# Making the gate tiles in one pass, and starting the first partial sums before the root is known

## The chip, the cores and the metric

The kernel runs on one core of a Trainium2 chip. It is written for five engines that run side by side: TensorE (PE in the profile, with its weight loads as PEld), VectorE (DVE), ScalarE (ACT), GpSimd (POOL) and SyncE (SP), which here only issues loads and stores. The metric is the time of one execution on the device in microseconds; lower is better. The median of three runs is compared.

## The reference

One step of a one-layer decoder for 256 prompt tokens and 8 groups of 4 sample tokens, 288 columns in all. Cut to what the change touches:

```python
mod = (silu(c) @ w_ada + b_ada).reshape(n, 6, 1, 2048)
sh_m, sc_m, gt_m, sh_f, sc_f, gt_f = [mod[:, i] for i in range(6)]
h = rms(x, g_mix) * (1 + sc_m) + sh_m
proj = h @ w_in                       # 2048 -> 9216 = 72 tiles of 128
b_gate, c_gate, hc, u, v, ga, gb = split(proj, [1024, 1024, 1024, 1024, 1024, 2048, 2048])
ya = b_gate * causal_conv(c_gate * hc)
yb = gelu(u) * spatial_mix(rms(gelu(v), g_v))
x = x + gt_m * ((sigmoid(ga) * (ya @ w_pa) + sigmoid(gb) * (yb @ w_pb)) @ w_out)
```

Behind it stand a second norm, a gated feed-forward layer of width 5632 and a last norm. `rms(x, g)` divides each token by the root of its mean square over 2048 features; that root is one number per token. Tokens lie along the columns: x is 16 feature tiles of 128 rows by 288 columns. There are nine conditioning vectors: one for the prompt, eight for the sample groups.

## The kernel before

Every large product is made in full fp32 accuracy from two rounded parts: a weight tile of 128x128 is split into `hi` (ACT, L331) and `lo` (VectorE, L333), the activations likewise, and each weight tile takes three matmuls (L344 to L346) of 288 columns.

Weights arrive in blocks of up to 1 MB, in one stream, in the order of the list `steps`. A block goes into one of RAW = 5 raw buffers; its load is issued when the block RAW places ahead of it in the stream is run, and waits on SP until that one's buffer is free (for a weight block: once its `lo` parts are made; for a conditioning block: once its matmuls are done). Blocks are split one ahead of use, in four buffers each for `hi` and `lo`.

Conditioning (`Ada`, L249) is made on TensorE in units: aA gives feature tile 0 of shift and scale, aB tiles 1 and 2, aC tiles 3 to 6, aD tile 7, aE tiles 8 to 15; a2 to a5 serve later stages. A block of it is four column groups of the array side by side (L274). `tail` copies a unit's sum out (L289), transposes it on TensorE (L293 or L298) and adds the bias (L302).

The product `h @ w_in` is split over features, because the conditioning arrives feature by feature. For all 72 output tiles:

- wA: feature 0, six blocks of 12 tiles; `sinkA` copies the 72 partial tiles out, on ACT and VectorE in turn (L434, L436).
- wB: features 1 and 2, nine blocks of 8 tiles; `sinkB` adds (L439).
- wC: features 3 to 7, 24 blocks of 3 tiles; `sinkB` again.
- wD: features 8 to 15, 36 blocks of 2 tiles; `sinkD` adds (L447) and goes on by tile number: 0 to 23 are the convolution's three parts, 24 to 31 u, 32 to 39 v, 40 to 71 the two gates (a tanh, L457).

Before wA come the loads of c, constants, x and aA in this order (L717 to L719), the squares of x (ACT, L150) and their sum (VectorE, L155), the root (`token_rstd3`: L167, a power on POOL, L171), its broadcast over partitions (L177), `norm1`, and `mk_h1(0, 1)`, which scales and shifts feature tile 0 (`modulate`: ACT L205, POOL L208 and L209, ACT L211, VectorE L216). The other 15 tiles are multiplied by the root on POOL (`norm1b`, L410).

The compiler of the program orders each engine's instructions by the program's order and by what it holds to be ready; `tc.issue_after(i)` puts an engine's instructions behind `i` on that engine, without a wait.

Of the kernel before, what the change touches and what calls it, by code (L numbers as in the profile page):

```python
# [10 lines left out]
P = 128  # L11
D = 2048
T = 288
# [6 lines left out]
SLOTS = 92  # L20
RAW = 5
# [24 lines left out]
    "wA": (0, 1, 12),  # L46
    "wB": (1, 2, 8),
    "wC": (3, 5, 3),
    "wD": (8, 8, 2),
# [12 lines left out]
def decoder_kernel(tc, d):  # L62
    nc = tc.nc
    from contextlib import ExitStack
# [12 lines left out]

def _body(tc, nc, d, pc, pw, pslot, ptmp, pps):
# [25 lines left out]
    SY.dma_start(ct, d["c"])  # L104
    cp1 = const("cp1", [P, C1_END])
    SY.dma_start(cp1, d["cpack1"])
# [7 lines left out]
    ident = cp[:, C_ID : C_ID + 128]  # L114
# [6 lines left out]
    def load_x():  # L121
        for a, b in ((0, 5), (5, 10), (10, 14), (14, 16)):
            SY.dma_start(x[:, a:b, :], d["x"][:, a:b, :])
        SY.dma_start(cp, d["cpack2"])
        SY.dma_start(masks[96:], d["cpack2"][:32, C_MASKS : C_MASKS + 32])
# [8 lines left out]
    A.activation(ctt, ct, AF.Tanh, scale=0.5)  # L134
    V.scalar_tensor_tensor(ctt, ctt, 1.0, ct, ALU.add, ALU.mult)
    V.tensor_scalar(cs[:, :, :NC], ctt, 0.5, None, ALU.mult)
# [7 lines left out]
    class SquareSum:  # L144
        def __init__(self):
            self.acc, self.last = None, None

        def add(self, a):
            q = tmp() if self.last is not None else ptmp.tile([P, T], F32, tag="acc", name=nm("acc"), bufs=1)
            A.activation(q, a, AF.Square)  # L150
            if self.last is not None:
                if self.acc is None:
                    self.acc = self.last
                else:
                    V.tensor_tensor(self.acc, self.acc, self.last, ALU.add)  # L155
            self.last = q
# [31 lines left out]
    def split(a, n=T):  # L188
        hi = slot(F32R, (P, n))
        A.copy(hi, a)  # L190
        lo = slot(F32R, (P, n))
        V.tensor_tensor(lo, a, hi.bitcast(F32), ALU.subtract)  # L192
        return hi, lo

    def normed(kt, rb):
        t = slot()
        V.tensor_tensor(t, x[:, kt, :], rb, ALU.mult)  # L197
        return t

    def modulate(ks, get, gm, sh0, out):  # L200
        hs, his = {}, {}

        def affine(k, t):
# [5 lines left out]
            G.tensor_tensor(sam(h[:, TP:]), sam(h[:, TP:]), bc4(mod[:, sh0 + k, 1:]), ALU.add)  # L209
# [34 lines left out]
    class Step:  # L244
        defer = False
        raw = None
        parts = None

    class Ada(Step):  # L249
# [15 lines left out]
        def run(self):  # L265
# [4 lines left out]
            for k in range(self.nk // ks):  # L270
                for j in range(4):
                    kt = self.blk * self.nk + k * ks + j % ks
                    o = (k * 4 + j) * w
                    self.last = PE.matmul(  # L274
                        acc[32 * j : 32 * j + 32, :w],
                        cs[:, kt, :],
                        self.raw[:, o : o + w],
                        start=(kt < ks),
                        stop=(kt >= 16 - ks),
                        tile_position=(0, 32 * j),  # L280
                        skip_group_check=True,
                    )
# [26 lines left out]
    class Blk(Step):  # L309
        def __init__(self, name, idx, rhs, sink):  # L310
            self.name, self.idx, self.rhs, self.sink = name, idx, rhs, sink
# [7 lines left out]
        def split(self, most=99):  # L319
# [4 lines left out]
            for s in range(len(self.parts), n, per):  # L324
# [6 lines left out]
                A.copy(hi, self.raw[:, s * 128 : e * 128])  # L331
# [5 lines left out]
        def run(self):  # L337
            for j in range(self.nm):
                ps = psmain()
                for k in range(self.nk):  # L340
# [3 lines left out]
                    PE.matmul(ps[:, :T], wh, ah, start=first, stop=False)  # L344
                    PE.matmul(ps[:, :T], wh, al, start=False, stop=False)  # L345
                    PE.matmul(ps[:, :T], wl, ah, start=False, stop=last)  # L346
                self.sink(self.idx * self.nm + j, ps)

# [37 lines left out]
    S = {}  # L386

    def squares1():
        ss = SquareSum()
        for k in range(16):  # L390
            ss.add(x[:, k, :])
        S["ss1"] = ss

    def rstd1():
        with tc.issue_after(aA[1].last.ins):
            S["r1"] = token_rstd3(S["ss1"], D)

    def norm1():
        with tc.issue_after(aA[3].last.ins):
            ps = rstd_bcast(S["r1"])  # L400
        with tc.issue_after(S["bc"].ins):
            aA[3].tail()
        S["rb1"] = ptmp.tile([P, T], F32, tag="rb", name=nm("rb"), bufs=1)
        A.copy(S["rb1"], ps)
        xn[0] = normed(0, ps)

    def norm1b():
        for k in range(1, 16):
            xn[k] = slot()
            G.tensor_tensor(xn[k], x[:, k, :], S["rb1"], ALU.mult)  # L410

    xn = {}
    h1 = {}

    def mk_h1(k0, k1):
        def f():
            V.scalar_tensor_tensor(  # L417
                gm1[:, k0:k1, :],
                mod[:, 16 + k0 : 16 + k1, :],
                1.0,  # L420
                gmix[:, k0:k1].unsqueeze(2).to_broadcast([P, k1 - k0, NC]),
                ALU.add,
                ALU.mult,
            )
            modulate(range(k0, k1), xn.pop, gm1, 0, h1)

        return Do(f)
# [3 lines left out]
    def sinkA(m, ps):  # L431
        part[m] = slot()
        if m % 2:
            A.copy(part[m], ps[:, :T])  # L434
        else:
            V.tensor_copy(part[m], ps[:, :T])  # L436

    def sinkB(m, ps):
        V.tensor_tensor(part[m], ps[:, :T], part[m], ALU.add)  # L439
# [5 lines left out]
    def sinkD(m, ps):  # L445
# [10 lines left out]
        elif m >= 40:  # L456
            A.activation(a, a, AF.Tanh, scale=0.5)  # L457
        elif m >= 16:
            mix_conv(m - 16)

# [116 lines left out]
    def sink_wo(m, ps):  # L577
# [8 lines left out]
        for k in range(2 * m - 16, 2 * m - 14) if m >= 8 else ():  # L586
            a = tmp(TU)
            A.activation(a[:, :TP], x[:, k, :TP], AF.Copy, scale=gm2[:, k, 0:1])
            G.tensor_tensor(sam(a[:, TP:T]), sam(x[:, k, TP:]), bc4(gm2[:, k, 1:]), ALU.mult)
            G.tensor_copy(a[:, T : T + NC], mod[:, 48 + k, :])  # L590
            G.memset(a[:, T + NC :], 0.0)
            xg[k] = split(a, TU)
# [77 lines left out]
    aA = ada("aA")  # L670
# [3 lines left out]
    wA = [Blk("wA", i, rh1, sinkA) for i in range(6)]  # L674
    wA[0].defer = True
    wB = [Blk("wB", i, rh1, sinkB) for i in range(9)]
    wC = [Blk("wC", i, rh1, sinkB) for i in range(24)]
    steps += weave(wA, visits(ada("aB"), 2, mk_h1(1, 3)), 1, 4)
    steps += weave(wB, visits(ada("aC"), 4) + visits(ada("aD"), 2, mk_h1(3, 8)), 0, 6)
    steps += weave(wC, visits(ada("aE"), 4, mk_h1(8, 16)), 2, 17)  # L680

    def wD(m0, m1):
        return [Blk("wD", i, rh1, sinkD) for i in range(m0 // 2, m1 // 2)]

    steps2 = wD(32, 40) + wD(24, 26) + [Do(v_stats)] + wD(26, 28) + [Do(v_transpose)] + wD(28, 32)
# [3 lines left out]
    steps2 += weave(wD(40, 72), [[spatial(g)] for g in range(8)], 2, 12)  # L689
    steps2 += [Blk("pa", i, ya.__getitem__, sink_pa) for i in range(8)]  # L690
# [26 lines left out]
    load_x()  # L717
    for s in stream[:AHEAD]:
        s.load()  # L719
    blks = [s for s in stream if isinstance(s, Blk)]  # L720
    nxt, cur = 0, 0
    for s in steps:
# [4 lines left out]
        if i + AHEAD < len(stream):  # L727
            stream[i + AHEAD].load()
# [122 lines left out]
```

## Time and profile before

| | |
|---|---|
| median of 3 runs | 1660.55 us (1659.83 to 1661.02) |
| the profiled execution | 1658.19 us, span 1656.2 us |
| granted TensorE clock, mean | 0.996 |
| moved by DMA | 357.59 MB, 216 GB/s over the span |

The span is what the trace covers. Busy time of TensorE is modelled from pipelined matmuls, so two that overlap count once; the number of matmuls in a stretch says more than the busy share. A row of the timeline has start, length, engine, line, operation, what is written and read, and the count of instructions that were merged; in square brackets stands the engine's idle time before it and what ended that.

### The profile page before, as it was taken

The numbers are of one execution on the slowest core, as the hardware profiler recorded it, in microseconds if no ns is written. First come the engines' busy times: TensorE is split into PE (matmuls) and PEld (weight loads), VectorE is DVE, ScalarE is ACT, GpSimd is POOL, SyncE is SP. The second block draws the span as 40 slices with busy tenths as digits, with TensorE's granted clock in tenths as the row PEclk, the third lists the DMA queues.
The fourth block names the chain that finished last, engine by engine and source line by source line (L and its number), as shares of the span: only waits on it lengthen the run. The fifth ranks groups of instructions, "written<-read, shape, count | busy, mean of one in ns | idle before, by whom it ended". The sixth has DMA issues, their size and how long they took to land.

```text
span 1656.2 us, 31141 instructions
## 1 busy us (share of the span) xinstructions
PE 1624.6 (98%) x12456; PEld 1556.0 (94%) x12456; DVE 995.4 (60%) x2034; ACT 736.2 (44%) x1371; POOL 63.9 (4%) x154
## 2 busy tenths in 40 slices
PE   5999999999999999999999999999999999999997
PEld 5889899989898999999999899999999999999997
DVE  5767556878755557557844455555555555555565
ACT  4534334643444434446733344444444444344453
POOL 3000001000000000002300000000000000000000
PEclk9999999999999999999999999999999999999998
DMA  7685786567777776674466755443454444645342
GB/s 267 254 335 207 277 313 246 191 233 261 277 308 277 282 286 251 251 263 154 152 255 254 304 170 196 171 163 137 158 206 163 168 141 156 204 161 171 126 170 76
DMA packets 56034, 357.59 MB, mean 216 GB/s; under 512 B 6369, under 2 KB 8577, under 8 KB 22737
## 3 DMA queue, kind: packets, MB, share of 16 engines
q1 hardware_dynamic: 55536, 354.88, 58.8%
q8 instruction: 97, 1.59, 0.4%
q0 software_dynamic: 352, 0.73, 0.1%
q14 instruction: 49, 0.39, 0.1%
HBM read 352.50 MB, written 3.09 MB: 215 GB/s over the span
## 4 chain that ended last, share of the span: by engine, by line
issue 50%; DVE 0%; ACT 0%; POOL 0%; PE 0%; POOLq 0%; DVEq 0%
DVE x L651 0%; PE px L177 0%; ACT t L205 0%; ACT s L211 0%; POOL t L208 0%; ACT hi L331 0%; POOL t L209 0%; POOLq L837 0%; DVE s L197 0%; DVE s L216 0%; DVEq L837 0%; POOLq L208 0%
## 5 line engine op out<-in xcount | busy, mean ns | idle before, releaser
L344 PE MATMUL pm<-s,hi 128*128 128x288 f32 x3712 | 1100.1, 297 | 7.2 <-ACT s L434 3.1
L345 PE MATMUL pm<-s,hi 128*128 128x288 f32 x3712 | 1097.1, 296 | 0.1
L346 PE MATMUL pm<-s,lo 128*128 128x288 f32 x3712 | 1094.1, 295 | 0.0
L331 ACT CAST hi<-raw 128x512 fp32r<-128x512 f32 (+1 forms) x966 | 581.9, 610 | 793.0 <-PE pm L345 661.7
L333 DVE TENSOR_TENSOR lo<-raw,hi 128x512 fp32r<-128x512 f32 (+1 forms) x966 | 652.5, 682 | 450.7 <-ACT hi L331 434.7
L344 PEld LDWEIGHTS pm<-s,hi 128*128 128x128 f32 x3712 | 698.8, 188 | 26.7 <-issue 14.6
L346 PEld LDWEIGHTS pm<-s,lo 128*128 128x128 f32 x3712 | 699.2, 188 | 0.2 <-DVE lo L333 0.2
L345 PEld LDWEIGHTS pm<-s,hi 128*128 128x128 f32 x3712 | 698.8, 188 | 0.5 <-DVE s L216 0.5
L274 PE MATMUL ada<-raw,cs 128*32 128x512 f32 (+2 forms) x960 | 91.1, 519 | 12.3 <-DMA raw<-in_aA 12.2
L439 DVE TENSOR_TENSOR s<-pm,s 128x288 f32<-128x288 f32 x144 | 64.3, 454 | 48.4 <-PE pm L346 48.2
L274 PEld LDWEIGHTS ada<-raw,cs 128*32 128x32 f32 x960 | 29.0, 113 | 56.4 <-issue 39.0
L447 DVE TENSOR_TENSOR s<-pm,s 128x288 f32<-128x288 f32 x72 | 32.8, 455 | 24.1 <-PE pm L346 23.8
L190 ACT CAST s<-t 128x288 fp32r<-128x288 f32 (+1 forms) x76 | 32.9, 432 | 21.0 <-DVE t L550 9.6
L192 DVE TENSOR_TENSOR s<-t,s 128x288 fp32r<-128x288 f32 (+1 forms) x76 | 34.8, 458 | 7.1 <-ACT s L190 7.0
L171 POOL TENSOR_TENSOR r<-r,mhalf 128x3 f32<-128x3 f32 x4 | 3.8, 957 | 908.2 <-DVE r L170 908.2
L232 DVE SCALAR_TENSOR_TENSOR x<-pm,mod,x 128x256 f32<-128x256 f32 x80 | 37.9, 474 | 0.0
L623 DVE SCALAR_TENSOR_TENSOR t<-t,pm 128x288 f32<-128x288 f32 x42 | 19.1, 454 | 25.3 <-PE pm L346 25.3
L231 DVE TENSOR_TENSOR t<-pm,mod 128x32 f32<-128x32 f32 x80 | 15.3, 191 | 29.6 <-PE pm L346 29.6
L155 DVE TENSOR_TENSOR acc<-acc,t 128x288 f32<-128x288 f32 x48 | 21.9, 456 | 12.3 <-ACT t L150 11.0
L150 ACT ACTIVATE t<-x 128x288 f32<-128x288 f32 x45 | 19.1, 442 | 21.3 <-DVE x L233 20.6
L457 ACT ACTIVATE s<-s 128x288 f32<-128x288 f32 x32 | 14.2, 445 | 14.2 <-DVE s L447 14.1
L208 POOL TENSOR_TENSOR t<-s,gm 128x32 f32<-128x32 f32 x32 | 11.3, 357 | 235.7 <-DVE gm L417 219.1
(114 smaller groups left out, 494.5 us busy)
## 6 DMA issues: line engine op xcount, KB each, us to landing
raw<-in_fi SPq DMA_DIRECT2D x84, 1024.0 KB, 4.8
raw<-in_a SPq DMA_DIRECT2D x64, 1024.0 KB, 6.4
raw<-in_f SPq DMA_DIRECT2D x64, 704.0 KB, 4.1
raw<-in_wD SPq DMA_DIRECT2D x36, 1024.0 KB, 6.3
raw<-in_wC SPq DMA_DIRECT2D x24, 960.0 KB, 6.2
raw<-in_aE SPq DMA_DIRECT2D x16, 1024.0 KB, 8.0
raw<-in_wo SPq DMA_DIRECT2D x16, 1024.0 KB, 7.2
raw<-in_wB SPq DMA_DIRECT2D x9, 1024.0 KB, 7.2
```

The source lines that it names most:

```text
L155: V.tensor_tensor(self.acc, self.acc, self.last, ALU.add)
L190: A.copy(hi, a)
L192: V.tensor_tensor(lo, a, hi.bitcast(F32), ALU.subtract)
L232: V.scalar_tensor_tensor(x[:, m, :TP], ps[:, :TP], mod[:, gt0 + m, 0:1], x[:, m, :TP], ALU.mult, ALU.add)
L274: self.last = PE.matmul(acc[32 * j : 32 * j + 32, :w], cs[:, kt, :], self.raw[:, o : o + w], start=(kt < ks), stop=(kt >= 16 - ks), tile_p ...
L331: A.copy(hi, self.raw[:, s * 128 : e * 128])
L333: V.tensor_tensor(lo, self.raw[:, s * 128 : e * 128], hi.bitcast(F32), ALU.subtract)
L344: PE.matmul(ps[:, :T], wh, ah, start=first, stop=False)
L345: PE.matmul(ps[:, :T], wh, al, start=False, stop=False)
L346: PE.matmul(ps[:, :T], wl, ah, start=False, stop=last)
L439: V.tensor_tensor(part[m], ps[:, :T], part[m], ALU.add)
L447: V.tensor_tensor(a, ps[:, :T], a, ALU.add)
```

## The change

**Tiles.** The 32 gate tiles (40 to 71) are no longer made in four parts. `late` makes each in one block of 1 MB over all 16 features with one sum in PSUM, and `sink_gate` takes the tanh straight out of PSUM. Tiles 0 to 39 (EARLY = 40) keep their four parts: wA is now five blocks of 8 tiles, wB five of 8, wC twenty of 2, and `Pair` loads the feature half 8 to 15 of two tiles out of the whole-tile array. In the later order, the first 16 gate tiles are woven with `spatial`, the others stand between pa and pb.

**The root.** wA and wB work on x times gain, without the root (`early`, `scaled`). Their activations have ten more columns (TU = 298): nine carry the shifts, in the form shift of the prompt and differences of the groups to it. So each partial tile also holds what the shift contributes. Once the root is known, `rescale` multiplies each of the 40 partial tiles by it on POOL (one operation on 288 columns, one on the 32 sample columns that adds the groups' difference), and `sinkC` adds the prompt's shift along with wC's sum. wC and later work on the true h (`mk_h1`), now multiplied by the root on VectorE in `normed`; features 0 to 2 of it are made during wD.

**Order.** aA is loaded first, x in four pieces: tile 0 behind aA, tiles 1 and 2 behind wA1, 3 to 8 behind wA4, 9 to 15 behind wB0, and the second constants behind that. The squares stand behind the last copy of wA on ACT, and POOL sums them; the root follows wB1 and four more of aC. Through wC TensorE's order is the program's (`in_order`, `behind`). 20 warm-up matmuls on ones fill the time before wA. `ident` becomes a tile of its own.

**Buffers.** RAW 5 to 6, slots 92 to 85.

```diff
-SLOTS = 92
-RAW = 5
+SLOTS = 85
+RAW = 6
+EARLY = 40
...
-    "wA": (0, 1, 12),
+    "wA": (0, 1, 8),
     "wB": (1, 2, 8),
-    "wC": (3, 5, 3),
-    "wD": (8, 8, 2),
+    "wC": (3, 5, 2),
+    "wD": (0, 16, 1),
...
+    def warm(n, after=None):
+        ps = psmisc()
+        with behind(after):
+            for _ in range(n):
+                PE.matmul(ps[:, :P], ones, ones, start=True, stop=True)
+
+    def scaled(k, gm, columns):
+        a = tmp(TU)
+        A.activation(a[:, :TP], x[:, k, :TP], AF.Copy, scale=gm[:, k, 0:1])
+        G.tensor_tensor(sam(a[:, TP:T]), sam(x[:, k, TP:]), bc4(gm[:, k, 1:]), ALU.mult)
+        columns(a[:, T : T + NC])
+        G.memset(a[:, T + NC :], 0.0)
+        return split(a, TU)
...
+    def early(k0, k1):
+        def f():
+            gain1(k0, k1)
+            for k in range(k0, k1):
+
+                def columns(t):
+                    G.tensor_copy(t, mod[:, k, :])
+                    G.tensor_tensor(t[:, 1:], t[:, 1:], t[:, 0:1].to_broadcast([P, NB]), ALU.subtract)
+
+                xe[k] = scaled(k, gm1, columns)
+            if k0 == 0:
+                wA[0].after, wA[0].lead = S["hi"], SEG
+
+        return Do(f)
+
+    def rescale(m0, m1):
+        def f():
+            for m in range(m0, m1):
+                a = part[m]
+                with behind(S.get("aff")):
+                    G.tensor_tensor(a[:, :T], a[:, :T], S["rb1"], ALU.mult)
+                G.tensor_tensor(sam(a[:, TP:T]), sam(a[:, TP:T]), bc4(a[:, T + 1 : T + NC]), ALU.add)
+
+        return Do(f)
...
+    def sinkC(m, ps):
+        a = part[m]
+        V.scalar_tensor_tensor(a[:, :T], ps[:, :T], a[:, T : T + 1], a[:, :T], ALU.add, ALU.add)
+        part[m] = a[:, :T]
...
+    def sink_gate(m, ps):
+        part[m] = slot()
+        A.activation(part[m], ps[:, :T], AF.Tanh, scale=0.5)
...
-    steps = [Do(squares1)] + aA[:2] + [Do(rstd1)] + aA[2:] + [Do(norm1)]
-    aA[3].defer = True
-    steps += [Do(lambda: wA[0].split(1)), mk_h1(0, 1), Do(lambda: wA[0].split()), Do(norm1b)]
...
-    steps += weave(wA, visits(ada("aB"), 2, mk_h1(1, 3)), 1, 4)
-    steps += weave(wB, visits(ada("aC"), 4) + visits(ada("aD"), 2, mk_h1(3, 8)), 0, 6)
-    steps += weave(wC, visits(ada("aE"), 4, mk_h1(8, 16)), 2, 17)
...
+    steps = [Do(silu), Do(lambda: warm(6))]
+    for s in aA:
+        steps += [s, Do(lambda s=s: warm(2, s.last))]
+    steps += [early(0, 1), Do(lambda: warm(6, aA[3].last)), wA[0], wA[1]] + aB[:2] + [wA[2]] + aB[2:]
+    steps += [wA[3], early(1, 3), wA[4], Do(squares1), wB[0]] + aC[:4] + [wB[1], Do(rstd1)] + aC[4:] + [Do(norm1)]
+    steps += [gain(3, 7), rescale(0, 8), wB[2], mk_h1(3, 4)] + aD + [gain(7, 8), wB[3], mk_h1(4, 6), wB[4]]
+    steps += [mk_h1(6, 8), rescale(8, 24), wC[0]] + aE[:4] + wC[1:4] + [rescale(24, EARLY)]
+    steps += aE[4:8] + wC[4:7] + aE[8:12] + wC[7:10] + aE[12:] + [gain(8, 16)] + wC[10:11]
+    for i in range(8):
+        steps += [mk_h1(8 + i, 9 + i), wC[11 + i]]
+    steps += wC[19:] + [Do(lambda: S.update(strict=False, pe=None))]
...
-    steps2 += weave(wD(40, 72), [[spatial(g)] for g in range(8)], 2, 12)
-    steps2 += [Blk("pa", i, ya.__getitem__, sink_pa) for i in range(8)]
+    steps2 += weave(late(40, 56), [[spatial(g)] for g in range(8)], 2, 13)
+    steps2 += [Blk("pa", i, ya.__getitem__, sink_pa) for i in range(8)] + late(56, 72)
...
-    load_x()
-    for s in stream[:AHEAD]:
+    aA[0].load()
+    SY.dma_start(ct, d["c"])
+    aA[1].load()
+    SY.dma_start(cp1, d["cpack1"])
+    for s in aA[2:]:
         s.load()
+    load_x(0, 1)
+    wA[0].load()
+    wA[1].load()
+    load_x(1, 3)
+    pieces = {wA[4]: (3, 9), wB[0]: (9, 16)}
```

More of the change, by code (lines that the diff above doesn't have):

```diff
@@ L273, in run @@
                     o = (k * 4 + j) * w
[L274 to L282, printed above, removed]
+                    with behind(S.get("pe")):
+                        self.last = in_order(
+                            PE.matmul(
+                                acc[32 * j : 32 * j + 32, :w],
+                                cs[:, kt, :],
+                                self.raw[:, o : o + w],
+                                start=(kt < ks),
+                                stop=(kt >= 16 - ks),
+                                tile_position=(0, 32 * j),
+                                skip_group_check=True,
+                            )
+                        )
             if (self.blk + 1) * self.nk == 16 and not self.defer:
```

147 lines of the change are left out of this document (81 added, 66 removed).

## The prediction

> **What bounds the kernel now.** I read the page first, then busy time by stretches, the waits of TensorE, and last the start of the timeline.
>
> ```profile
> span 1656.2 us, 31141 instructions
> ...
> PE 1624.6 (98%) x12456; PEld 1556.0 (94%) x12456; DVE 995.4 (60%) x2034; ACT 736.2 (44%) x1371; POOL 63.9 (4%) x154
> ```
> ```profile
> 0.00:23.40 23.40, 8.57 (x84) 7.05 (x84) 9.11 (x28) 9.85 (x24) 2.41 (x9) 1.00 0.92 363
> 23.40:40.00 16.60, 14.15 (x76) 13.05 (x77) 14.36 (x22) 8.67 (x20) 13.88 (x14) 0.90 0.41 147
> 40.00:140.00 100.00, 96.94 (x873) 89.27 (x873) 76.27 (x166) 45.87 (x93) 3.37 (x14) 1.00 0.76 287
> 140.00:1640.00 1500.00, 1500.00 (x11397) 1442.15 (x11396) 889.33 (x1806) 670.80 (x1234) 43.41 (x117) 1.00 0.58 210
> 1240.00:1280.00 40.00, 40.00 (x304) 40.00 (x304) 20.86 (x34) 17.99 (x32) 0.00 (x0) 1.00 0.48 164
> ```
>
> Columns: stretch, its length, then busy time and count of PE, PEld, DVE, ACT, POOL, granted clock, DMA share, GB/s. From 140 to 1640 us TensorE is never idle. There an edit pays only if it removes TensorE instructions, and this one removes none. So all that can be won lies before 140. I count it with the steady price of a matmul, 40.00/304 = 0.1316 us.
>
> ```profile
> 0.00:140.00 140.00, 69.60 (x228) 43.75 (x228) 0.99 0.74 283
> ```
> ```profile
> 23.40:140.00 116.60, 13.14 (x256) 7.51 (x256) 0.99 0.71 267
> ```
> ```profile
> 85.31 3.66 PE L274 MATMUL ada<-raw,cs 128*32 128x256 f32 x64
> ```
>
> The first row counts L344 alone, one of three matmuls per weight tile: 3 x 228 = 684 matmuls, 90.0 us. The second counts conditioning matmuls (L274) after the first unit: 256 records. A record 256 wide costs 3.66/64 = 0.057 us; 192 are that wide (11.0 us), 64 half as wide (1.8 us), and the 64 of aA cost 1.8 us too. Root and transposes I put at 3.2 us (the six-record groups L167 twice and L177 below, halved for full clock, and a little more). Useful work: 90.0 + 11.0 + 1.8 + 1.8 + 3.2 = 107.8 us, so TensorE **loses 32.2 us** before 140. Most of it lies at the front:
>
> ```profile
> 2.60 0.32 ACT L134 ACTIVATE ctt<-ct 128x144 f32<-128x144 f32 x1 [0.58 <-DMA ct<-in_c]
> ...
> 12.17 2.27 PE L274 MATMUL ada<-raw,cs 128*32 128x128 f32 x32 [12.17 <-DMA raw<-in_aA]
> ...
> 14.71 1.44 PE L167 MATMUL px<-ones,acc 128*128 128x1 f32 x6 [0.27 <-DVE acc L155]
> ...
> 16.01 1.42 PE L167 MATMUL px<-ones,t 128*128 128x1 f32 x6
> ...
> 19.22 1.65 PE L177 MATMUL px<-cp,r 128*128 128x128 f32 x6
> 19.36 0.27 ACT L289 COPY ev<-ada 128x128 f32<-128x128 f32 x1 [6.48 <-PE ada L274]
> ...
> 20.66 0.45 PE L298 MATMUL px<-cp,ev 128*128 128x18 f32 x2
> ...
> 21.44 0.45 DVE L197 TENSOR_TENSOR s<-x,px 128x288 f32<-128x288 f32 x1
> 21.93 0.60 ACT L205 ACTIVATE t<-s,mod,gm 128x256 f32<-128x256 f32 x1 [0.62 <-DVE s L197]
> ...
> 23.42 1.33 PE L344 MATMUL pm<-s,hi 128*128 128x288 f32 x4 [2.30 <-ACT s L211]
> ```
> ```profile
> PE ada L274 <- DMA raw<-in_aA: 12.2, 1, 12.2
> PE pm L344 <- ACT s L434: 3.1, 2, 2.3
> ...
> PE pm L344 <- DVE s L436: 1.5, 1, 1.5
> ```
>
> The first main matmul starts at 23.42: x is loaded ahead of aA (first wait 12.2 us), and root and norm stand before it.
>
> **The front after the change.** aA is loaded first. Two rows price that: the latency of a small load, and the rate of a full queue.
>
> ```profile
> ct<-in_c SPq DMA_DIRECT2D x1, 72.0 KB, 1.8
> ```
> ```profile
> 8.00:12.00 4.00, 0.00 (x0) 0.00 (x0) 3.26 (x8) 3.52 (x10) 0.00 (x0) 1.00 1.03 412
> ...
> 16.00:20.00 4.00, 4.00 (x42) 3.50 (x43) 0.32 (x2) 0.27 (x1) 0.85 (x1) 1.00 1.02 418
> ...
> 28.00:32.00 4.00, 2.54 (x12) 2.30 (x13) 3.06 (x6) 0.56 (x2) 4.00 (x5) 0.79 0.57 199
> ...
> 60.00:64.00 4.00, 1.72 (x12) 1.36 (x11) 2.61 (x6) 2.89 (x8) 0.71 (x4) 1.00 1.01 391
> ```
>
> The first aA block (512 KB) lands near 0.7 + 1.8 + 1.3 = 3.8 us, ct just behind; silu takes about 1 us from landing (0.32 on ACT, two short DVE steps), so L274 can start at 5.2. The fourth block lands near 8.2. Four blocks at half clock cost 2.27/2 = 1.1 us each, and the two warm-up matmuls between blocks up to 2 x 1.65/3 = 1.1 us; aA thus ends between 9.3 (loads decide) and 13.0 (everything queues cold). I take 11.5, in between. From the copy of aA's sum (19.36) to the first main matmul (23.42) it was 4.06 us; 0.8 of that was L298 queued behind L177, 0.5 was L197, and neither is left on this path. The scaling adds small POOL steps (some 0.3). So 3.1, and 0.4 for warm-ups that may stand ahead of the transposition: first main matmul at **15.0** (bounds 12.5 and 17.0).
>
> The 20 warm-ups use time in which TensorE waits anyway. Without that cover they cost 20 x 0.28 = 5.5 us at full clock (half of L177's 0.55 each). What they may buy is the clock: from 23.4 to 40 it was granted 0.90 on average, so 1.7 of the 32.2 us went there, in rows such as 28 to 32 with 0.79.
>
> **The extra columns.** 40 tiles x 3 features x 3 = 360 matmuls become 298 wide.
>
> ```profile
> 799.87 0.30 PE L360 MATMUL pm<-s,hi 128*128 128x298 f32 x1
> ...
> 801.82 0.30 PE L362 MATMUL pm<-s,lo 128*128 128x298 f32 x1
> ```
>
> Fourteen steps between these rows: 0.139 us each, 0.0077 more than 0.1316, so **2.8 us**. Nothing hides it.
>
> **Loads against TensorE up to wB2.** The new order has fewer main blocks early (wA 40 tiles for 72, wB 5 blocks for 9) for the same 14 conditioning blocks of 1 MB after aA. Up to the third wB block the queue must bring aA 2.1, wA 2.6, wB 3.1, aB and aC 12.6, x 2.4, and 0.5 of constants: 23.3 MB, at 0.415 MB/us 56 us from about 3, so wB2 lands at 59. One cast and one subtraction (0.6 + 0.7 and a wait) later it can start: 60.5. TensorE in the same order: 15.0 + 5 wA at 3.3 (24 x 0.139) + 4 aB at 0.9 + wB0 at 6.7 = 41.8; aC3 lands at 44, done 45; wB1 lands at 46.6, starts 48.0, ends 54.7; root 1.4; four aC to 59.8; broadcast 0.8: **60.6**. Both say 60.6: loads and TensorE are about even here. TensorE's order is fixed up to the end of wC, so a late operand holds back everything behind it, rstd1 and the broadcast among it; the one late load that I find is wB1's, 3 us.
>
> That wait bears on the clock. A wait of 2.6 us stood in before's row 60 to 64 with the clock at 1.00 through it. The Trainium skill (TensorE: Matmul & The Clock Gate, "What's actually happening") says that an idle window of about 3.4 us throttles the array to half rate for a further window; by it the wait could cost another 1.7 us, and the sum would stand that much higher.
>
> **POOL against VectorE from wB2 to wC0.** Squares' sums and the multiplication of 40 partial tiles by the root go to POOL. What POOL does to VectorE, the trace shows at the start, where L410 runs:
>
> ```profile
> 22.49 14.79 POOL L410 TENSOR_TENSOR s<-x,rb 128x288 f32<-128x288 f32 x15
> ```
> ```profile
> 24.73 4.89 DVE L333 TENSOR_TENSOR lo<-raw,hi 128x512 fp32r<-128x512 f32 x4
> 29.55 1.18 DVE L436 COPY s<-pm 128x288 f32<-128x288 f32 x3
> ```
> ```profile
> 119.70 2.49 DVE L333 TENSOR_TENSOR lo<-raw,hi 128x512 fp32r<-128x512 f32 x4
> ...
> 129.97 1.18 DVE L439 TENSOR_TENSOR s<-pm,s 128x288 f32<-128x288 f32 x3
> ```
>
> A subtraction takes 4.89/4 = 1.22 us beside POOL and 0.62 alone; copies out of PSUM keep their 0.39. For L439 (one operand in PSUM, one in SBUF) beside a wide POOL operation there is no row: bounds 0.39 and 0.99, and I take 0.39, as it is nearer to the copies. The Trainium skill (SBUF — State Buffer, "Who interferes with whom") says that only a VectorE instruction with two SBUF inputs fights GpSimd's reads; by it the sum stays.
>
> Between 60.6 and wC0 VectorE must do 13 subtractions (8.1), 24 sums (9.4), ten steps of mk_h1 for features 3 to 7 (3.9) and small things (0.6): 22.0 us. rescale(0,8) holds POOL for 8 x (0.99 + about 0.36) = 10.8 us, in which some seven subtractions pay 0.6 more: 26.2 us. TensorE needs 3 x 6.7 + 1.8 = 21.9. So VectorE is late, wC0 waits, by 4.3 us: it starts at **86.8**. During squares (wB0) the same fight is covered by the wait for wB1. In wC, VectorE needs per block 2.5 subtractions and 2 sums, 2.3 us of 4.0; beside POOL 3.8: no wait, 1 us allowed.
>
> **What costs nothing.** Gate tiles lose three of four evacuations (L434 or L436, L439 twice) on ACT and VectorE; past 140 TensorE is full either way. mk_h1(0) to (2) move behind wC, where a full TensorE covers them; without cover each costs about 0.9 us. sinkC adds the shift in the sum that sinkB made anyway. Loads in halves (Pair) have 6.3 us of TensorE per MB as cover. 85 slots hold 80 at the peak (h1 32, ya 16, yb 16, gates 16).
>
> **Sum.** By 86.8 the change has done 360 main matmuls (47.4 us at the old price), conditioning 14.6 and 3.2: 65.2. Lost 21.6, with the 1 us in wC 22.6, the extra columns included. Gain 32.2 - 22.6 = 9.6. The profiled execution took 1658.19 us (span 1656.2 and 2.0 around it), so 1648.6. The median of the three runs, 1660.55, lies 2.4 above it: **1651**.
>
> **Rivals.** *No wait behind the front* (VectorE is never late, wB1 comes in time): 7 us better, 1644. For it: VectorE's 22.0 equals TensorE's 21.9 when POOL stays out of its way. Against: POOL can only run then.
>
> *The loads do not stream*, the slower side. Each load waits for a buffer, and over 40 us before moved far less than its peak:
>
> ```profile
> 0.00:40.00 40.00, 22.73 (x160) 20.10 (x161) 23.47 (x49) 18.52 (x43) 16.29 (x22) 0.96 0.71 273
> 40.00:80.00 40.00, 37.72 (x315) 35.04 (x315) 31.20 (x66) 23.48 (x51) 0.85 (x4) 1.00 0.70 257
> 80.00:120.00 40.00, 39.24 (x363) 34.82 (x361) 27.39 (x61) 11.49 (x21) 0.00 (x0) 1.00 0.86 337
> ```
>
> At 0.337 MB/us wB2 lands at 3 + 69 = 72, starts 73.5, 13 us late: 1664. Below 0.36 the gain is gone, below 0.34 it is a loss. Against it: the low rows are of a queue without free buffers, the 4-us rows with a queue of work all show 391 to 418. The Trainium skill (DMA: Bandwidth & Descriptors, "Specifications") gives about 358 GB/s as the limit from HBM for a core, which by the same sum would make 1660; the rows above it contradict it here.
>
> *POOL also slows L439 and its like*: 0.6 for some 12 of them in wB2 to wB4, 7 us: 1658, no measurable change. *The early start is not early*: aA ends at 13, the clock stays at half into wA: 5 us worse, 1656.
>
> **Chances.** Forecast 0.50 (own range 1646 to 1656), no wait 0.17, loads 0.12, POOL on sums 0.11, late start 0.10. A measurement tells 0.2%, 3.3 us, from no change. Faster: 0.50 + 0.17 + 0.08 of the late start + 0.04 of POOL + 0.01 of the loads = 0.80; same 0.02 + 0.06 + 0.02 = 0.10; slower 0.09 of the loads and 0.01 of POOL = 0.10. The range 1643 to 1661 leaves out the worst loads and the best of no wait.
>
> **What would show it.** First main matmul at 15 against 23.42; clock 1.00 from there; wB2 near 60 and wC0 near 87; waits of TensorE for loads about 3 us before wB1 and for VectorE some 4 us in wB; subtractions near 1.2 us under rescale; TensorE full again from there. Wrong if the first matmul is later than 17, if loads average under 0.36 MB/us up to 60, or if TensorE shows new gaps after 140.

## The result, and the profile after

The changed kernel takes **1661.69 us** (median of 12 runs, 1659.50 to 1662.58), the kernel before 1660.12 in the same session (12 runs, 1658.17 to 1661.34): a ratio of **1.0008, 95% interval 0.9999 to 1.0017**. That is no measurable change. The forecast was 1651, faster.

The page of the changed kernel:

```profile
span 1659.7 us, 31274 instructions
...
PE 1631.3 (98%) x12496; PEld 1562.2 (94%) x12496; DVE 963.6 (58%) x1931; ACT 736.3 (44%) x1365; POOL 116.4 (7%) x245
```

The profiled execution took 1661.62 us. TensorE has 40 instructions more (the 20 warm-ups, two each), VectorE 103 fewer and ACT 6 fewer. Busy time by stretches, columns as in the prediction:

```profile
0.00:14.20 14.20, 11.02 (x106) 8.82 (x106) 1.92 (x9) 3.25 (x7) 0.94 (x9) 0.88 0.89 337
14.20:40.00 25.80, 22.54 (x179) 19.30 (x179) 16.38 (x35) 14.71 (x35) 1.12 (x7) 0.93 1.00 399
40.00:92.00 52.00, 44.40 (x405) 38.83 (x404) 30.66 (x67) 20.86 (x46) 27.34 (x44) 0.90 0.81 322
92.00:140.00 48.00, 47.58 (x369) 39.09 (x367) 32.11 (x54) 12.70 (x24) 38.22 (x62) 1.00 0.78 305
140.00:1640.00 1500.00, 1497.46 (x11383) 1448.31 (x11384) 874.49 (x1750) 682.34 (x1251) 47.87 (x123) 1.00 0.58 206
```

From 140 us on TensorE is full but for 2.5 us. Before that there is a hole, from 14 to 92 us: 10.9 us without a matmul, and a granted clock of 0.93 and 0.90, where before's rows from 40 on had 1.00. What TensorE waited for from 0 to 92 us (total, times, longest):

```profile
PE pm L375 <- ACT s L496: 2.8, 2, 1.9
PE pm L375 <- ACT hi L361: 2.7, 3, 1.2
PE pm L375 <- DVE s L501: 2.6, 1, 2.6
PE pm L377 <- DVE lo L363: 1.6, 3, 0.8
...
PE ada L302 <- DMA raw<-in_aA: 0.2, 1, 0.2
```

L375 to L377 are the three matmuls (L344 to L346 before). No wait behind the front is TensorE's own wait for a load: all that add up to more than half a microsecond are for casts (L361), subtractions (L363) and copies or sums out of PSUM (L496, L501) by ACT and VectorE. When the first matmul of each block starts, in us, forecast and in the trace (the last two columns are kernels of the experiments below):

| block | forecast | after | e3_rescale | e7_all |
|---|---|---|---|---|
| wA0, the first | 15.0 | 14.23 | 12.91 | 14.58 |
| wB0 (15.0 + 5 x 3.3 + 4 x 0.9) | 35.1 | 41.87 | 42.05 | 39.29 |
| wB1 | 48.0 | 53.42 | 53.62 | 49.59 |
| wB2 | 60.6 | 70.28 | 70.49 | 62.97 |
| wC0 | 86.8 | 100.53 | 94.31 | 86.69 |

The whole miss is made before wC0: 13.7 us there, 13.0 at the end (1661.62 against 1648.6). From wA0 to wC0 the trace has 86.3 us. Taking the distance from each matmul's start to the next, and from it the steady 0.139 (main), 0.057 or 0.03 us (conditioning), **65.7 us are work, 14.1 are in 15 waits, 5.9 are matmuls at a low clock** (the last 0.6 are many distances a little above the steady ones). The forecast had 66.2 of work here (47.4 + 2.8 + 14.6 + 3.2, less 1.8 for aA) in 71.8 us: the work was right, and 5.6 us were left for waiting (the waits that it names, 3 and 4.3 us, make 7.3), where 20.0 came.

**What held the operands back.** In the timeline (start, length, engine and line; in brackets the idle time ahead and its releaser) four places show one pattern. First, ACT in wA1 and the matmul that waited:

```profile
16.77 0.41 ACT L496 COPY s<-pm 128x298 f32<-128x298 f32 x1 [0.39 <-PE pm L377]
20.07 0.62 ACT L361 CAST hi<-raw 128x512 fp32r<-128x512 f32 x1 [2.89 <-DMA raw<-in_wA]
20.59 0.40 ACT L496 COPY s<-pm 128x298 f32<-128x298 f32 x1
```
```profile
21.05 0.59 PE L375 MATMUL pm<-s,hi 128*128 128x298 f32 x1 [1.88 <-ACT s L496]
```

A cast of wA2 stands in ACT's queue ahead of the copies of wA1. Its load lands at 20.0, so ACT sits idle for 2.89 us, the sums of wA1 stay in PSUM, and TensorE has no free sum to write to. A load does stop TensorE, through ACT. Second, wB1:

```profile
50.65 0.44 ACT L153 ACTIVATE t<-x 128x288 f32<-128x288 f32 x1 [0.45 <-POOL acc L158]
51.54 0.44 ACT L153 ACTIVATE t<-x 128x288 f32<-128x288 f32 x1 [0.45 <-POOL acc L158]
52.42 0.44 ACT L153 ACTIVATE t<-x 128x288 f32<-128x288 f32 x1 [0.44 <-POOL acc L158]
52.77 2.17 ACT L361 CAST hi<-raw 128x512 fp32r<-128x512 f32 x4
```
```profile
53.42 0.40 PE L375 MATMUL pm<-s,hi 128*128 128x298 f32 x1 [1.18 <-ACT hi L361]
```

All 16 squares (L153) stand ahead of the casts of wB1. POOL sums them one per 0.89 us, and each square waits for POOL, so the casts start at 52.77 with no wait of their own, though the load landed at 49.2. Third, wB2:

```profile
67.74 0.37 ACT L318 COPY ev<-ada 128x256 f32<-128x256 f32 x1 [12.81 <-PE ada L302]
69.31 0.40 ACT L448 COPY rb<-px 128x288 f32<-128x288 f32 x1 [1.20 <-PE px L180]
69.61 2.18 ACT L361 CAST hi<-raw 128x512 fp32r<-128x512 f32 x4
```
```profile
70.28 0.41 PE L375 MATMUL pm<-s,hi 128*128 128x298 f32 x1 [1.01 <-ACT hi L361]
```

ACT was idle for 12.81 us, in which wB2 landed (62.0), and yet its casts start at 69.61: a copy of TensorE's own late result stands ahead. Fourth, in wB2, across three engines:

```profile
69.79 2.29 POOL L480 TENSOR_TENSOR s<-s,rb 128x288 f32<-128x288 f32 x2 [4.56 <-ACT rb L448]
...
79.74 0.24 POOL L234 TENSOR_TENSOR t<-t,mod 128x32 f32<-128x32 f32 x1
```
```profile
80.02 0.43 ACT L236 CAST s<-t 128x288 fp32r<-128x288 f32 x1 [7.73 <-POOL t L234]
```
```profile
70.26 4.22 DVE L363 TENSOR_TENSOR lo<-raw,hi 128x512 fp32r<-128x512 f32 x4
74.40 1.25 DVE L501 TENSOR_TENSOR s<-pm,s 128x298 f32<-128x298 f32 x3
80.48 0.46 DVE L241 TENSOR_TENSOR s<-t,s 128x288 fp32r<-128x288 f32 x1 [4.83 <-ACT s L236]
80.86 0.46 DVE L501 TENSOR_TENSOR s<-pm,s 128x298 f32<-128x298 f32 x1
```
```profile
81.38 0.40 PE L375 MATMUL pm<-s,hi 128*128 128x298 f32 x1 [2.60 <-DVE s L501]
```

rescale(0, 8) (L480, L481) holds POOL from 69.79 to 79.8. Behind it stands L234, a quarter of a microsecond for mk_h1(3, 4); ACT's L236 waits 7.73 us for that, VectorE's L241 waits 4.83 us for L236, and behind L241 stands a sum out of PSUM that TensorE needs. Nothing in that chain is needed before wC. VectorE did not run out of time; it sat idle.

**The clock.** Rows over three of the waits' sequels:

```profile
55.20:58.50 3.30, 3.30 (x16) 3.30 (x15) 3.25 (x5) 0.00 (x0) 1.27 (x2) 0.51 1.00 422
72.30:75.70 3.40, 3.40 (x16) 3.40 (x16) 3.35 (x6) 0.00 (x0) 3.40 (x6) 0.50 0.98 409
82.60:86.00 3.40, 3.35 (x64) 2.90 (x56) 2.52 (x7) 2.05 (x5) 0.99 (x4) 0.51 0.29 39
```

Half the clock, 3.4 us at a time, and so once more at 21.1 us: 13.7 us in all from wA0 to wC0, each behind waits that add up to 1.7 to 2.6 us.

### The profile page after: what moved, and what is told of

It is laid out like the page before. It is cut to its first block, busy times and chain, and to the rows that moved or that the text cites. A ratio compares the mean times of both kernels' runs of the same rounds, so it can differ in the third digit from the quotient of the medians.

```text
span 1659.7 us, 31274 instructions
## 1 busy us (share of the span) xinstructions
PE 1631.3 (98%) x12496; PEld 1562.2 (94%) x12496; DVE 963.6 (58%) x1931; ACT 736.3 (44%) x1365; POOL 116.4 (7%) x245
## 4 chain that ended last, share of the span: by engine, by line
issue 51%; PE 43%; DMA 2%; POOL 1%; DVE 1%; ACT 1%; POOLq 0%; SPq 0%; DVEq 0%; ACTq 0%
PE pm L375 13%; PE pm L377 13%; PE pm L376 13%; PE ada L302 4%; DMA raw<-in_wC 1%; DVE lo L363 1%; DMA raw<-in_wA 1%; ACT hi L361 0%; POOL acc L158 0%; POOL s L480 0%; ACT t L230 0%; DMA raw<-in_aA 0%; DVE x L715 0%; ACT s L236 0%; PE px L170 0%
## 5 line engine op out<-in xcount | busy, mean ns | idle before, releaser
L375 PE MATMUL pm<-s,hi 128*128 128x288 f32 (+1 forms) x3712 | 1100.0, 296 | 9.4 <-ACT hi L361 3.6
L377 PE MATMUL pm<-s,lo 128*128 128x288 f32 (+1 forms) x3712 | 1096.0, 295 | 2.5 <-DVE lo L363 2.5
L376 PE MATMUL pm<-s,hi 128*128 128x288 f32 (+1 forms) x3712 | 1097.3, 296 | 0.4 <-DVE s L195 0.4
L363 DVE TENSOR_TENSOR lo<-raw,hi 128x512 fp32r<-128x512 f32 (+2 forms) x970 | 664.9, 688 | 547.0 <-ACT hi L361 531.9
L361 ACT CAST hi<-raw 128x512 fp32r<-128x512 f32 (+2 forms) x970 | 587.1, 608 | 794.1 <-PE pm L376 763.6
L375 PEld LDWEIGHTS pm<-s,hi 128*128 128x128 f32 x3712 | 699.7, 189 | 28.1 <-issue 13.8
L377 PEld LDWEIGHTS pm<-s,lo 128*128 128x128 f32 x3712 | 699.6, 188 | 3.9 <-DVE lo L363 3.9
L220 POOL TENSOR_TENSOR t<-x,gm 128x32 f32<-128x32 f32 x19 | 8.1, 429 | 423.8 <-DVE gm L652 378.4
L480 POOL TENSOR_TENSOR s<-s,rb 128x288 f32<-128x288 f32 x40 | 36.0, 902 | 4.6 <-ACT rb L448 4.6
L505 DVE SCALAR_TENSOR_TENSOR s<-pm,s 128x288 f32<-128x288 f32 x40 | 20.5, 514 | 17.1 <-PE pm L377 16.4
L153 ACT ACTIVATE t<-x 128x288 f32<-128x288 f32 x45 | 19.5, 444 | 23.8 <-DVE x L258 20.2
L230 ACT ACTIVATE t<-s,mod,gm 128x256 f32<-128x256 f32 x32 | 18.6, 597 | 7.4 <-DVE s L200 6.2
L241 DVE TENSOR_TENSOR s<-t,s 128x288 fp32r<-128x288 f32 x32 | 15.1, 478 | 10.4 <-ACT s L236 10.4
```

The costliest lines, as they stand in the source:

```text
L363: V.tensor_tensor(lo, self.raw[:, s * 128 : e * 128], hi.bitcast(F32), ALU.subtract)
L375: PE.matmul(ps[:, : self.n], wh, ah, start=first, stop=False)
L376: PE.matmul(ps[:, : self.n], wh, al, start=False, stop=False)
L377: self.last = in_order(PE.matmul(ps[:, : self.n], wl, ah, start=False, stop=last))
L480: G.tensor_tensor(a[:, :T], a[:, :T], S["rb1"], ALU.mult)
L505: V.scalar_tensor_tensor(a[:, :T], ps[:, :T], a[:, T : T + 1], a[:, :T], ALU.add, ALU.add)
```

## The experiments

The theory: each wait is one late instruction ahead of a ready one in an engine's queue, and moving that instruction takes the wait away. Rivals: VectorE has too much to do (the prediction's own reason); the low clock is the loss, whatever the waits; the gate tiles cost what the early start gains.

**rescale behind what waits for it (e3_rescale).** The same work on every engine, in another order:

```diff
-    steps += [gain(3, 7), rescale(0, 8), wB[2], mk_h1(3, 4)] + aD + [gain(7, 8), wB[3], mk_h1(4, 6), wB[4]]
-    steps += [mk_h1(6, 8), rescale(8, 24), wC[0]] + aE[:4] + wC[1:4] + [rescale(24, EARLY)]
+    steps += [gain(3, 7), wB[2], mk_h1(3, 4)] + aD + [gain(7, 8), wB[3], mk_h1(4, 6), wB[4]]
+    steps += [mk_h1(6, 8), rescale(0, 24), wC[0]] + aE[:4] + wC[1:4] + [rescale(24, EARLY)]
```

> The multiplication of tiles 0 to 7 by the root moves from ahead of mk_h1(3) to behind mk_h1(7) on POOL. Theory (mk_h1's small POOL steps wait behind 9.5 us of rescale, ScalarE's cast waits for them, VectorE's subtraction of it stands ahead of sums out of PSUM, and TensorE runs out of PSUM): the wait of 2.9 us near 80 us and the half clock behind it are gone, 4 us off the changed kernel. Rival (my prediction: VectorE has too much to do between wB2 and wC0, since subtractions cost 1.2 us beside POOL): the subtractions of wB2 get cheaper but those of wC0 to wC3 dearer, TensorE waits elsewhere for VectorE, within 1.5 us of the changed kernel.

Measured: 1654.31 us, ratio to before 0.9961 (0.9949 to 0.9974), 7.4 us better than after, where the theory had 4. VectorE in this kernel:

```profile
70.47 2.59 DVE L363 TENSOR_TENSOR lo<-raw,hi 128x512 fp32r<-128x512 f32 x4
72.98 1.21 DVE L501 TENSOR_TENSOR s<-pm,s 128x298 f32<-128x298 f32 x3
74.11 0.45 DVE L241 TENSOR_TENSOR s<-t,s 128x288 fp32r<-128x288 f32 x1
74.55 0.47 DVE L501 TENSOR_TENSOR s<-pm,s 128x298 f32<-128x298 f32 x1
```

L241 comes at 74.11 without a wait, and wC0 starts 6.2 us earlier (the table above), though wB2 starts as late as in after. Of this the four subtractions take 2.59 instead of 4.22 us; the rest is L241's idle time. From wB2 to wC0 it takes 23.8 us for 30.2, and 22.1 of them are matmuls: VectorE has time enough.

**The squares behind the casts of wB1 (e2_squares).** The last eight squares are put behind ACT's last cast of wB1:

```diff
-        for k in range(16):
+        for k in range(8):
...
+    def squares1b():
+        for k in range(8, 16):
+            with behind(wB[1].hi_last):
+                S["ss1"].add(x[:, k, :])
```

> Squares of features 8 to 15 go behind the casts of wB1 on ScalarE; in the changed kernel all 16 squares, paced by the sums on POOL, stand ahead of these casts. Theory (an instruction that is late holds back ready ones behind it on its engine): the casts start near 49.5 us, when wB1 has landed, in place of 52.8; wB1 follows aC without a wait; 2.6 us of idle time and 1.5 us of half clock go, 4 us off the changed kernel if the waits behind it stay. Rival (VectorE or the loads set the pace up to wC0): the wait before wB1 goes and comes back before wB2 or wC0, within 1 us of the changed kernel.

Measured: 1657.64 us, 0.9983 (0.9974 to 0.9992). ACT:

```profile
50.30 2.18 ACT L361 CAST hi<-raw 128x512 fp32r<-128x512 f32 x4 [4.28 <-DMA raw<-in_wB]
```

Now the casts start when the load lands, the waits before wB1 are gone, and wB2 starts at 67.2 for 70.3. The wait for VectorE in wB2 grew from 2.6 to 3.6 us: TensorE comes earlier to an instruction that is late by POOL. By the medians 4.1 us were kept, as the theory had it.

**The casts of wB2 ahead of the two copies (e5_cast), and the same with e3_rescale (e9_cast_rescale).**

```diff
-            A.copy(ev[:, :w], acc[:, :w])
+            with behind(S.get("cast")):
+                A.copy(ev[:, :w], acc[:, :w])
...
-        A.copy(S["rb1"], ps)
+        with behind(S.get("cast")):
+            A.copy(S["rb1"], ps)
...
```

`cast` is the last cast of wB2.

> ScalarE makes the casts of wB2 ahead of the copies of aC's sum and of the root's broadcast; in the changed kernel they stand behind both and start at 69.6 us, though wB2 landed at 62. Theory (order on an engine, then the clock): the casts are done by 66, wB2 starts right behind the broadcast near 69, 1.5 to 2 us of idle time and perhaps the half clock behind it go: 2 to 3.5 us off. Rival (loads or VectorE set the pace up to wC0): within 1 us of the changed kernel.

> The casts of wB2 early and rescale(0, 8) late, together; alone the first gained nothing (1.3 us worse than the changed kernel), the second 7.4. Theory: alone, the early casts only led sooner into the wait behind rescale; with that one gone they gain 2 to 3 us, 1652. Rival (the casts are of no account, loads set wB2): as with the late rescale alone, 1654, or 1 us worse.

Measured: e5_cast 1662.96 us, 1.0011 (1.0002 to 1.0020), 1.3 worse than after, where 2 to 3.5 better was forecast. wB2 starts at 67.9, 2.4 us earlier than in after, and from 60 to 92 us TensorE has one wait left:

```profile
PE pm L376 <- ACT hi L362: 5.9, 1, 5.9
```

The wait has moved on to the next casts, which stand behind mk_h1's steps on ACT and so behind the same L236. With rescale moved as well, e9_cast_rescale takes 1652.62 us, 0.9956 (0.9942 to 0.9969): 10.3 better than e5_cast. Alone the edit is of no use; on top of e3_rescale it brings 1.7 us by the medians, which the two intervals leave open; in the traces wC0 starts at 92.51 for 94.31.

**The casts of wA2 behind the copies of wA1 (e6_front).**

```diff
-    wA[0].defer = wA[1].defer = True
+    wA[0].defer = wA[1].defer = wA[2].defer = True
...
+    steps += [Do(lambda: wA[2].__dict__.update(after=evA[15])), wA[2]] + aB[2:]
```

> The casts of wA2 go behind ScalarE's last copy of wA1, alone on the changed kernel; there they stand in the midst of these copies and hold them until wA2 lands at 20 us. Theory (order on an engine, then the clock): the wait of 2 to 4 us near 21 us goes, and perhaps the half clock behind it: 2 to 4 us off at main matmul number 100, of which the wait before wB1, for casts behind squares that POOL paces, takes a part back, since that one ends at a fixed time: 0 to 2 us off at the end. Rival (the loads set the pace from the start): main matmul number 100 comes no earlier.

Measured: 1659.16 us, 0.9995 (0.9986 to 1.0003), 2.5 better than after. TensorE from 17 to 40 us:

```profile
PE pm L375 <- ACT s L496: 3.7, 2, 2.8
```

The wait at 21 us is gone and one of 2.8 us stands at 28.0, where the copies of wA2 stand behind casts of the next block, whose load had not landed. Main matmul number 100 comes at 36.46 for 37.33, 0.9 us sooner where 2 to 4 were forecast, though the first one came 1.75 sooner in this execution. Loads set this stage as much as ACT's order does.

**All four (e7_all).**

> All four reorderings on the changed kernel: squares 8 to 15 behind the casts of wB1, casts of wB2 ahead of the copies, rescale(0, 8) late, casts of wA2 behind the copies of wA1. Theory: the changed kernel's loss is made of these waits and the half clock behind them; 1647 to 1651, faster than both kernels, with no more than one half-clock stretch between 15 us and the end of the last main matmul. Rival (VectorE or the loads set the pace up to wC0): no better than the late rescale alone, 1654.

Measured: **1652.27 us** (1649.08 to 1652.77), **0.9946 (0.9933 to 0.9958)**, faster than both kernels, the median a little above the 1647 to 1651 expected. Its rows for 14.2 to 92 us:

```profile
14.20:40.00 25.80, 23.68 (x198) 20.13 (x197) 18.74 (x41) 16.32 (x39) 1.12 (x7) 1.00 1.01 403
40.00:92.00 52.00, 50.48 (x493) 44.98 (x495) 36.96 (x85) 24.52 (x53) 24.29 (x38) 1.00 0.89 356
```

88 matmuls more from 40 to 92 us than in after, TensorE idle for 1.5 us instead of 7.6, and the clock at 1.00 throughout. The waits from wA0 to wC0, counted in the same way, sum to some 5 us for 14.1, and wC0 starts at 86.69, where the forecast had it at 86.8.

**Filling the waits (e1_fill, e10_fill4).** Matmuls on constants are put into TensorE's queue where it waits, so that its clock is kept and no operand comes sooner: at two places (before wB1 and wB2), and at four (in wA1 and before block 7 of wB2 too).

```diff
+    def fill(n):
+        ps = psmisc()
+        for _ in range(n):
+            with behind(S["pe"]):
+                in_order(PE.matmul(ps[:, :P], ones, ones, start=True, stop=True))
...
```

> Ten matmuls on ones stand before wB1 and six before wB2, in the time in which TensorE waits for their weight parts. Nothing else is moved, so both waits stay as long as in the changed kernel. Theory (a wait on TensorE costs twice, once as idle time and once as the 3.4 us at half clock that follow it): the half-clock stretches near 55 and 72 us are gone, and 1.5 us each is saved, less up to 1 us of matmuls that outlast the wait: 2 to 3 us off the changed kernel. Rival (the waits alone cost the time, the clock is of no account since TensorE would wait for VectorE or a load anyway): the same time as the changed kernel, or 1 us more.

> The kernel after, with matmuls on constant operands put into TensorE's queue at the four places where it waits for over 2 us: 10 in wA1 before its second block of features, 10 before wB1, 6 before wB2, 12 before block 7 of wB2. Nothing that TensorE waits for comes earlier; the waits stay, but are filled. Theory that the low granted clock behind a wait is a cost of its own: the half-clock stretches at 21, 55, 72 and 82 us are gone, and 4 to 6 us come off the kernel after (1661.7): about 1656 to 1658. Rival, that the time goes with the late operands alone and the clock is a by-product: no change against the kernel after, or slower where the filling is longer than the wait.

Measured: e1_fill 1659.13 us, 0.9993 (0.9984 to 1.0002), 2.6 better than after, as its theory had it; e10_fill4 **1663.66 us**, 1.0019 (1.0011 to 1.0028), 2.0 worse, where 4 to 6 better was forecast. In e1_fill wB1 starts at 54.63, 1.2 us later than in after, since the fillers outlast the wait, and yet ends at 62.00 for 62.85: here the low clock had cost time of its own. In e10_fill4 the low stretches of after are gone up to 84 us, as meant. (In the traced execution the loads were late ahead of any filler, wA2's at 22.0 for 20.0, so of the filler in wA1 nothing is read.) Yet from wB2's first matmul (70.27) to the first of wB3 (86.61) it took 16.3 us, and 16.2 in after with 6.8 us at half clock. First after, then e10_fill4, conditioning matmuls and what follows:

```profile
82.40 3.55 PE L302 MATMUL ada<-raw,cs 128*32 128x128 f32 x64
86.44 0.40 PE L375 MATMUL pm<-s,hi 128*128 128x298 f32 x1 [0.49 <-ACT hi L361]
```
```profile
82.31 1.96 PE L309 MATMUL ada<-raw,cs 128*32 128x128 f32 x64
86.61 0.41 PE L384 MATMUL pm<-s,hi 128*128 128x298 f32 x1 [2.35 <-ACT hi L368]
```

At full clock they end 1.7 us sooner, and TensorE waits 1.9 us longer for the same cast. Behind that wait the low clock came after all, from 87.35 to 94.18, now in a place where nothing covers it, and wC0 starts at 104.08 for 100.53 in after:

```profile
88.00:92.00 4.00, 3.67 (x15) 3.67 (x16) 3.20 (x10) 1.94 (x5) 2.03 (x4) 0.50 0.50 106
```

So a half clock costs what the late operands leave uncovered: nothing from 72 to 86 us in after, part of its time in wB1, all of it behind 87 us in e10_fill4. The fillers leave the operands as late as they were, and the two kernels differ in sign; the rival that the low clock is the loss, whatever the waits, does not hold for most of it.

**The gate tiles alone (e8_gates).** The kernel before, with the 32 gate tiles in one pass (`late`, `Pair`, `sink_gate`; wA, wB and wC of 40 tiles) and root and order as they were:

```diff
-    "wA": (0, 1, 12),
+    "wA": (0, 1, 8),
...
-    "wC": (3, 5, 3),
-    "wD": (8, 8, 2),
+    "wC": (3, 5, 2),
+    "wD": (0, 16, 1),
...
```

> The gate tiles in one pass alone, on the kernel before: wA, wB and wC of 40 tiles, x, root and norm, five raw buffers and 92 slots as before. Theory (the new order of the start lost the time, not the gate tiles): first main matmul at 23.4 as before; fewer main matmuls stand between the same 14 conditioning blocks of 1 MB, so TensorE may wait some microseconds for loads before wC; from 140 us on full: 0 to 4 us slower than before. Rival (the gate part is what costs, the early start gains): 6 us slower or more.

Measured: **1671.78 us, 1.0069 (1.0057 to 1.0082)**, 12 us slower than before: the theory's 0 to 4 missed, and the rival's 6 or more came. Its rows:

```profile
40.00:140.00 100.00, 93.28 (x810) 82.92 (x803) 60.27 (x129) 36.15 (x74) 6.94 (x14) 0.95 0.77 286
140.00:200.00 60.00, 55.88 (x417) 45.18 (x417) 30.87 (x66) 23.43 (x49) 4.96 (x16) 1.00 0.91 347
```

Before had TensorE idle for 3.1 us from 40 to 140 and not at all behind it. Here it is 6.7 and 4.1, with a clock of 0.95 in the first row (half clock for 10.2 us in all, so some 5 us lost). The stream has the same conditioning blocks and fewer main matmuls beside them. The waits are spread over copies out of PSUM (2.5 us), casts (2.3), one load of aC (1.8), the scaled features (1.7) and smaller ones, so which of them comes of that is not shown; and the places of the conditioning blocks were chosen anew for 40 tiles, so another placing may cost less. So the rest of the change, taken together, is worth 10.1 us (1671.78 to 1661.69), a little less than the 11.7 that the gates cost on the old order: two large effects that cancel, not an edit without effect. In that sense the rival that the gate tiles cost what the early start gains holds beside the theory.

**Two waits more (e11_waits).** e7_all, with the first root's matmuls put two conditioning blocks later and the transposes of aE's last block behind one more block of wC:

```diff
-    steps += [wA[3], early(1, 3), wA[4], Do(squares1), wB[0], Do(squares1b)] + aC[:4] + [wB[1], Do(rstd1), Do(lambda: S.update(cast=wB[2].hi_last))] + aC[4:] + [Do(norm1)]
+    steps += [wA[3], early(1, 3), wA[4], Do(squares1), wB[0], Do(squares1b)] + aC[:4] + [wB[1], Do(lambda: S.update(cast=wB[2].hi_last))] + aC[4:6] + [Do(rstd1)] + aC[6:] + [Do(norm1)]
-    steps += aE[4:8] + wC[4:7] + aE[8:12] + wC[7:10] + aE[12:] + [gain(8, 16)] + wC[10:11]
+    steps += aE[4:8] + wC[4:7] + aE[8:12] + wC[7:10] + aE[12:] + wC[10:11] + [Do(late_tail), gain(8, 16)]
...
```

> The kernel e7_all (1652.3) with two of its remaining waits taken away: the root of the first token tile (wait of 1.46 us at 58) is put behind POOL's sums by one more block of matmuls, and the transposes of the last block of features of the gates (waits of 1.3 and 1.0 us at 143 and 145) are put off behind one more block. Theory that each wait is one instruction placed ahead of its operand: both waits go, and 1.5 to 3.7 us come off, 1648.5 to 1651. Rival, that what follows is bound by the other engines, so the wait comes back at the next instruction: within 1 us of e7_all.

Measured: 1651.10 us (1649.15 to 1653.06), 0.9940 (0.9926 to 0.9953): the interval is that of e7_all. The two waits are gone; in their place the profiled execution (1653.06 us) has waits of 1.2 us at 128.7 and at 148.2 for casts, and a half clock from 131.0 to 134.4. In this execution the rival holds: behind wB, the next cast was late too.

## Why the prediction was wrong, point by point

- **The front: right.** First main matmul at 14.23 for 15.0 (12.48 to 15.17 in the traces of the experiments on this kernel).
- **The loads: nearly right.** Where the queue was full (share near 1) the rows above have 399 to 422 GB/s, for the 415 taken. It was not always full: 22.84 MB came up to 60 us, 381 GB/s on average, and wB1 landed at 49.2 for 46.6, wB2 at 62.0 for 59. The rival "the loads do not stream" fell.
- **The extra columns and the work: right.** 65.7 us for 66.2.
- **POOL against VectorE, the prices: right.** A subtraction beside rescale took 4.22/4 = 1.06 us for the 1.22 taken, L501 stayed at 1.25/3 = 0.42, rescale(0, 8) took 10.0 for 10.8. But it met four subtractions, not seven: 1.6 us more for the 4.2 taken. The rival "POOL also slows L439" fell. The Trainium skill's rule (SBUF — State Buffer, "Who interferes with whom") agrees with both rows; it names VectorE's two-port modes as a second case, and says that `tensor_tensor`, the operation here, has none.
- **The waits: wrong, and this is the step that failed.** The prediction said: "TensorE's order is fixed up to the end of wC, so a late operand holds back everything behind it", found one late load worth 3 us, and 4.3 us for a VectorE with 26.2 us of work in 21.9. It applied the fixed order to TensorE alone. For ACT, VectorE and POOL it added up durations, as if each did what was ready. In this trace they run their queues in order too, and the edit put a slow or late instruction ahead of a needed one four times. VectorE's 26.2 us was not the bound: in that very stretch it sat idle for 4.83 us at L241, three times the 1.6 us that the slowed subtractions cost it, and in e3_rescale the wait is gone with the same instructions in another order. The prediction did price rescale's ten microseconds on POOL, and never asked what is queued behind it. The Trainium skill (PSUM — Partial Sum Buffer, "Engine vs sequencer instructions") calls these three engines' queues strictly first in, first out; by L236 and L241 above this case agrees.
- **The clock: present, and left out of the sum.** Of the 5.9 us that slow matmuls took, e10_fill4 shows the 2.8 from 72 to 86 us (wB2 and aD) to be covered by late operands, so they don't simply add to the waits. The Trainium skill's rule that the prediction quotes (TensorE: Matmul & The Clock Gate, "What's actually happening") gives windows of about 3.4 us, and the low stretches here last that long. It puts an idle window of that length ahead of them; here 1.7 to 2.6 us of waiting were enough. Two readings of before were off. Its wait in the row 60 to 64 is 2.28 us, not 2.6. And its rows print 1.00 up to the first change that the trace records, at 26.92, though its matmuls follow each other at 0.24 us until 26.71, about half the steady pace: the warm-ups could win more than the 1.7 us counted.
- **The gates: no price of their own.** The prediction counts fewer main blocks beside the same loads, and no loss beyond that; e8_gates shows 12 us on the old order. What they cost on the new order no run has apart.
- **A sign of being wrong came:** "TensorE shows new gaps after 140". There were 2.5 us of them, for none before; with wC0 13.7 us late and the end 13.0, they are not the miss.
- **Where the rest stands.** Without the four misplacements the profiled execution takes 1649.16 for the forecast 1648.6, and the median 1652.27 for 1651. That the numbers meet so well is luck in part. In e7_all wB2 starts at 62.97 for 60.6, and from there to wC0 it takes 23.7 us for 26.2: the loss to VectorE that the forecast had there did not come (TensorE waits 0.5 us). And the profiled execution lies 3.1 us below its kernel's median. So e7_all shows that the order was the loss, not that every term was right.

Not tried: the early start with all 72 tiles in four parts, which would need more slots than there are. What each of the four edits is worth alone stays loose, since they add to 12.7 us by the medians (4.1, 7.4, 2.5 and -1.3) and to 9.4 together: a wait that is removed is in part found again at the next late operand.

## What to carry to other kernels

A sum of durations per engine tells only that an engine could be in time. For every step that is moved or added, write down what stands behind it in that engine's queue and when that is needed; an instruction that waits for a distant engine, ahead of a copy out of PSUM or a cast of the next weights, stops TensorE though all engines have spare time. And when a wait is removed, look at the next late operand before counting the gain.

## What the hardware showed that was not expected

- POOL pays for the fight with VectorE as well. While the four subtractions ran (70.26 to 74.48), rescale's wide operation took 1.25 us and its narrow one 0.69; from 74.55 on, 0.80 and 0.24:

```profile
72.69 1.25 POOL L480 TENSOR_TENSOR s<-s,rb 128x288 f32<-128x288 f32 x1
73.89 0.69 POOL L481 TENSOR_TENSOR s<-s 128x32 f32<-128x32 f32 x1
74.55 0.80 POOL L480 TENSOR_TENSOR s<-s,rb 128x288 f32<-128x288 f32 x1
75.31 0.24 POOL L481 TENSOR_TENSOR s<-s 128x32 f32<-128x32 f32 x1
```

- About half a window of idle time was followed by a whole window at half clock, and where the windows lie differs from execution to execution. In each trace the changes of the granted clock lie whole multiples of 3.413 us apart (in after at 4.05, 7.46, 10.87, 21.11, 24.53, 55.25, 58.66, 72.31, 75.73, 82.55 and 85.97 us). Cut at these marks, the twelve traces up to 160 us have 23 such windows of 3.413 us at full clock in which TensorE sat idle for 1.73 us or more, by the profile; 22 of them were followed by a window at half clock (the exception is e5_cast from 76.18 to 79.59 us, idle for 2.00). Of those with 1.6 us or less none was; at 1.66 and 1.67 us it went either way. This tells apart waits that look alike: the two before wB1 in after (1.18 and 0.77 us) fall into one window, while before's wait of 2.28 us at 60.4 falls into two, with 0.62 and 1.67 us, and its clock stayed at 1.00. In other executions the marks lie elsewhere (the first at 8.85 in e10_fill4, at 10.38 in e7_all), so the same wait can cost a half clock in one and not in another.
